# A decoder trunk's feed-forward: down as seven products, on PSUM chains of two banks a half

## The chip, the cores and the metric

One core of a Trainium2 chip runs the whole kernel in one launch. The metric is the device time of that launch in microseconds (us). PE is the matrix engine, DVE the vector engine, ACT the scalar engine, POOL the GpSimd engine, and SP the engine whose queue issues most loads. Each runs its own instructions in the order in which they were built.

## The reference

One step of a two-layer decoder: layer 0 mixes tokens by an mLSTM, layer 1 by latent attention, and each layer ends in a SwiGLU feed-forward with residual. There are 1024 prompt tokens and 8 sample tokens, which the kernel takes together (T = 1032). The change touches the feed-forward alone:

```python
D_MODEL = 1024
D_FF = 2816
def swiglu(x, w_gate_up, w_down):
    g, u = jnp.split(x @ w_gate_up, 2, axis=-1)
    return (jax.nn.silu(g) * u) @ w_down
...
hp = hp + swiglu(rmsnorm(hp, norm_ffn[layer]), ffn_w_gate_up[layer], ffn_w_down[layer])
hs = hs + swiglu(rmsnorm(hs, norm_ffn[layer]), ffn_w_gate_up[layer], ffn_w_down[layer])
```

All data are float32.

## The kernel before

**Precision.** Every float32 operand of a matmul is split into a high part (rounded by ACT) and a low part (the rest, subtracted by DVE or POOL): `split`. One product is then three matmuls, high by high, high by low, low by high: `mm3`. The letters h and l at the end of a tile's name are these parts.

**Gate and up.** The 2816 hidden rows are 22 blocks of 128. For one block `f`, the weights are two raw tiles of 128 by 1024 (gate `a11, a12` and up `a21, a22`, by even and odd rows of the model dimension). The tokens are cut into two halves `i` (512 and 520), each half into two quarters of 256 or 260. `forms` makes seven combinations of the normalised activations once a layer, `operands` makes seven of the weights for each block (sums on POOL: `L1000` to `L1009`), and `gate_up` multiplies them pair by pair: seven products take the place of eight (a fast matrix product of two by two blocks). Each product is 4 x 3 matmuls of 256 or 260 columns. Then the quarters are put together by additions on DVE, `silu` on ACT, and the product with up: tile `u`, which is split into `ah`, `al`.

**Down.** The hidden blocks are taken in pairs (`f0`, `f0 + 1`), since each pair's result is added to the residual `x_d` in memory by an accumulating DMA. `down` is a generator: one step is one chunk of 344 tokens of one output tile (`d` of 8), 2 blocks x 3 matmuls, then an eviction to `st` by ACT; after three chunks POOL issues the accumulating DMA. 24 steps are a pair. `gate_up` of the next blocks calls `next(down)` after each half product, which lays the down matmuls between the gate matmuls on PE.

**The edges.** In each layer blocks 0 and 1 run for half 0 ahead of the loop as plain products (`gate_up_half`, in `out_proj`) and for half 1 inside `ffn`. The last four blocks are not in the loop's down but in the products that follow: `to_mla` in layer 0, `finish` in layer 1, where the last gate block is also run one half after the other, so that half 0 can go on.

**What sets the order.** The program is recorded through pools of tiles with a fixed number of buffers (`bufs`), and instructions are placed on each engine's list by a scheduler at build time. At run time each engine follows its list and waits on semaphores. PSUM has eight banks under three names, `sc` (4), `mm` (2) and `ss` (2).

## Time and profile before

| | us |
|---|---|
| median of 3 runs (lowest, highest) | 2751.73 (2743.95, 2754.61) |
| the profiled execution | 2762.2 |
| its span | 2760.4 |
| PE busy | 2588.2 (94%) |
| DVE, ACT, POOL busy | 1495.5, 1178.5, 876.8 |

The first feed-forward runs from about 540 to 1250 us of the span, the second from about 2030 to the end. In the profile's rows, a group is a line of the code, an engine, an operation, `out<-in` tile names and the shape, then a count, the busy time and the mean ns of one, and behind the second bar the engine's idle time just before and what ended it. In a timeline row the first number is the start and the second the duration, both in us. Line numbers are those of the kernel before; the same helpers stand three lines lower in the changed one (`L131` is `L134` there, `L115` is `L118`).

### The profile page before, as it was taken

The page shows a single profiled execution, that of the slowest core. Times are in us where ns is not written, and L with a number is a line of the kernel's source. Part 1 is how long each engine was busy: PE and PEld are TensorE (multiplying, and loading weights), DVE is VectorE, ACT ScalarE, POOL GpSimd, SP SyncE. Part 2 cuts the span into 40 slices and gives each one's busy share as a digit, 9 for nine tenths or more (in the row PEclk, how much of TensorE's full clock was granted, in tenths as well). Part 3 has the DMA queues.
Part 4 walks back from the last instruction along what each step waited for, and adds up shares of the span by engine and source line. Part 5 has one row for each costly group of instructions (what it writes and reads, how often), then busy time and mean ns, then how long its engine had stood idle before and what let it go on. Part 6 is the DMA issues. An engine that isn't in the chain of part 4 may idle for free.

```text
span 2760.4 us, 52158 instructions
## 1 busy us (share of the span) xinstructions
PE 2588.2 (94%) x20719; PEld 2438.5 (88%) x20719; DVE 1495.5 (54%) x3217; ACT 1178.5 (43%) x2651; POOL 876.8 (32%) x846
## 2 busy tenths in 40 slices
PE   8999988989999999999988888798989999999998
PEld 8998977989999999999875667676888999999998
DVE  4345668863343443366557776677574444434445
ACT  4212334444444444443344455446344444444443
POOL 1001002233333333332334444442223333333343
PEclk9999989999999999999989999999999999999999
DMA  5133454526566556552666766654533666565653
GB/s 184 39 76 93 124 143 116 158 58 129 119 123 122 116 114 125 101 163 96 230 222 237 245 231 218 217 202 123 176 102 88 126 117 122 119 118 117 118 129 112
DMA packets 345210, 384.29 MB, mean 139 GB/s; under 512 B 24601, under 2 KB 296350, under 8 KB 336646
## 3 DMA queue, kind: packets, MB, share of 16 engines
q0 software_dynamic: 41088, 183.34, 27.7%
q1 hardware_dynamic: 279478, 181.26, 22.5%
q10 hardware_dynamic: 24400, 16.36, 2.4%
q8 instruction: 163, 2.67, 0.4%
q14 instruction: 81, 0.66, 0.1%
HBM read 255.17 MB, written 125.70 MB: 138 GB/s over the span
## 4 chain that ended last, share of the span: by engine, by line
PE 69%; DVE 13%; DMA 8%; ACT 4%; issue 4%; POOL 2%; another core or an unknown queue 0%; SPq 0%; ACTq 0%; POOLq 0%; DVEq 0%
PE sc L133 10%; PE sc L131 10%; PE sc L132 9%; PE mm L131 5%; PE mm L133 5%; PE mm L132 5%; PE ss L131 5%; PE ss L132 5%; PE ss L133 5%; DMA Gb<-G_d 2%; DVE tt L1700 2%; PE ss L1732 2%; PE ss L1707 2%; DVE wl L115 2%; PE mm L1603 1%
## 5 line engine op out<-in xcount | busy, mean ns | idle before, releaser
L131 PE MATMUL ss<-ah,dh 128*128 128x344 f32 x864 | 276.7, 320 | 6.0 <-ACT st L1075 5.6
L1075 ACT COPY st<-ss 128x344 f32<-128x344 f32 x432 | 190.2, 442 | 211.8 <-PE ss L133 182.5
L132 PE MATMUL ss<-al,dh 128*128 128x344 f32 x864 | 276.7, 320 | 1.9 <-POOL al L115 1.9
L133 PE MATMUL ss<-ah,dl 128*128 128x344 f32 x864 | 275.9, 319 | 0.0
L114 ACT ACTIVATE wh<-wr 128x512 fp32r<-128x512 f32 (+2 forms) x152 | 126.0, 830 | 229.0 <-PE mm L132 132.9
L1077 POOL DMA_DIRECT2D x_d<-st x144 | 125.4, 871 | 237.1 <-ACT st L1075 230.1
L131 PEld LDWEIGHTS ss<-ah,dh 128*128 128x128 f32 x864 | 162.5, 188 | 7.0 <-ACT st L1075 6.1
L115 POOL TENSOR_TENSOR al<-u,ah 128x512 fp32r<-128x512 f32 (+1 forms) x84 | 118.4, 1410 | 146.5 <-ACT ah L114 146.3
L132 PEld LDWEIGHTS ss<-al,dh 128*128 128x128 f32 x864 | 162.7, 188 | 2.4 <-POOL al L115 2.4
L115 DVE TENSOR_TENSOR wl<-S,wl 128x512 fp32r<-128x512 f32 x89 | 77.4, 870 | 158.0 <-ACT wl L114 130.3
L133 PEld LDWEIGHTS ss<-ah,dl 128*128 128x128 f32 x864 | 162.3, 188 | 0.0
L1700 DVE STREAM_TRANSPOSE tt<-nat 128x1024 f32<-128x1024 f32 x128 | 154.1, 1223 | 12.1 <-PE ss L1707 8.0
L1041 DVE TENSOR_TENSOR u<-u,sc 128x260 f32<-128x260 f32 (+1 forms) x168 | 70.7, 421 | 115.4 <-PE sc L133 114.1
L115 DVE TENSOR_TENSOR wh<-S,wh 128x512 fp32r<-128x512 f32 x91 | 68.2, 749 | 118.7 <-ACT wh L114 90.8
L115 DVE TENSOR_TENSOR wl<-wr,wh 128x1024 fp32r<-128x1024 f32 (+2 forms) x83 | 100.1, 1206 | 43.1 <-ACT wh L114 35.8
L1007 POOL TENSOR_TENSOR S<-S,wr 128x512 f32<-128x512 f32 x45 | 62.9, 1398 | 174.4 <-DVE wl L115 88.1
L1000 POOL TENSOR_TENSOR S<-wr 128x512 f32<-128x512 f32 x45 | 62.0, 1378 | 168.3 <-DMA wr<-in_ffn_w_gate_up_dram 157.7
L131 PE MATMUL mm<-zh,wh 128*128 128x344 f32 x320 | 105.3, 329 | 8.5 <-DVE ot L459 8.5
L1707 PE MATMUL ss<-tt,qbd 128*32 128x128 f32 x2560 | 95.4, 285 | 16.2 <-DVE tt L1700 10.9
L115 DVE TENSOR_TENSOR dl<-dr,dh 128x256 fp32r<-128x256 f32 x144 | 69.2, 481 | 71.4 <-ACT dh L114 71.4
L133 PE MATMUL mm<-zh,wl 128*128 128x344 f32 x320 | 104.5, 327 | 0.0
L132 PE MATMUL mm<-zl,wh 128*128 128x344 f32 x320 | 104.5, 327 | 0.0
(920 smaller groups left out, 9243.9 us busy)
## 6 DMA issues: line engine op xcount, KB each, us to landing
x_d<-st POOLq DMA_DIRECT2D x144, 516.0 KB
wr<-in_ffn_w_gate_up_dram SPq DMA_DIRECT2D x98, 512.0 KB
dr<-in_ffn_w_down_dram SPq DMA_DIRECT2D x144, 128.0 KB
wr<-in_mlstm_w_in_dram SPq DMA_DIRECT2D x24, 512.0 KB
wr<-in_mlstm_w_out_dram SPq DMA_DIRECT2D x16, 512.0 KB
wr<-in_mla_w_o_dram SPq DMA_DIRECT2D x15, 512.0 KB
q<-qn_d SPq DMA_DIRECT2D x28, 256.0 KB
x_d<-x SPq DMA_DIRECT2D x16, 260.0 KB
```

What stands on the lines that cost most here:

```text
L114: ins = nc.scalar.activation(hi, src, AF.Copy)
L115: self.low = e.tensor_tensor(lo, src, hi.bitcast(F32), op=ALU.subtract)
L131: mm(ps, wh, xh, start=start, stop=False, **kw)
L132: mm(ps, wh, xl, start=False, stop=False, **kw)
L133: self.last = mm(ps, wl, xh, start=False, stop=stop, **kw)
L1000: G(s, a21, a22, op=ALU.add)
L1007: G(s, s, a11, op=ALU.subtract)
L1041: V.tensor_tensor(u[:, 1], u[:, 1], ps, op=ALU.add)
L1075: nc.scalar.copy(st[:, cs], ps)
L1077: nc.gpsimd.dma_start(self.x_d[:, d], st, accum_op=ALU.add)
L1700: V.transpose(out=tt, in_=src.rearrange("p s (c i) -> p c s i", i=32))
L1707: nc.tensor.matmul(psS[32 * j:32 * j + 32, u * P:u * P + P], self.qbd[:, b, cb], tt[:, c, 4 * j:4 * j + 4].rearrange("p s k -> p (s k)"), ...
```

## The change

Down is now made by seven products too, for a pair of blocks and two output tiles (`dp` of 4) at a time. For this each pair's `u` (two blocks x two quarters of a half) is turned into seven sums, one tile each (`b0` to `b6` and the half's number), and the down weights into seven (`dA` to `dD`, two forms in each but `dD`). The scheme is the one of `PRODUCTS`, now used for gate and for down: two PSUM banks a half, products 0, 3, 2 and 5 in bank 0 and 4, 1 and 6 in bank 1. Inside a bank a product may add to what the one before left, and after it the bank is copied out as one of the four outputs. A down step is one product of one half, 3 matmuls of 256 or 260 columns; 14 steps are a group (`dp`), 56 a pair. A group ends in one accumulating DMA a half (2 x 512 or 2 x 520 columns). `SPREAD` says at which step of a pair each activation sum (`t1` to `t4`, in place in `u`) and each form of the next pair is made: entries 44 to 55 run in the last 12 steps of the pair before, and 56 to 60 in its own first five.

The loop's down now takes ten pairs a layer, and only the last two blocks are left to `to_mla` and `finish`. `gate_up` calls the down generator twice a half product. Weight forms of gate rotate through three buffers (`wh` twice, `w3`), not four; raw tiles have two (`wr`), not three; the two `wl` buffers now hold down's results of half 0.

```diff
-PRODUCTS = ((0, "a", 1), (1, "b", 1), (4, "a", 0), (2, "c", 1), (5, "b", 0), (3, "d", 1), (6, "c", 0))
-BANK = {"a": "sc", "b": "sc", "d": "sc", "c": "mm"}
+PRODUCTS = ((0, 0, 1), (4, 1, 1), (3, 0, 0), (1, 1, 1), (2, 0, 0), (5, 0, 0), (6, 1, 0))
+PARTS = {0: ("A", 0), 4: ("A", 1), 3: ("B", 0), 1: ("B", 1), 2: ("C", 0), 5: ("D", 0), 6: ("C", 1)}
+SPREAD = ((44, 0, 0), (45, 0, 1), (45, "t1", 0), (46, "t1", 1), (48, 4, 0), (49, 1, 0), (50, 1, 1), (51, 4, 1),
...
+          (56, 2, 1), (57, 5, 0), (58, 6, 0), (59, 5, 1), (60, 6, 1))
...
     def operands(self, wg, f):
...
         G(s, a21, a22, op=ALU.add)
         G(s3, a11, a21, op=ALU.subtract)
         yield put(a11)
+        yield put(a12)
+        s1 = put(s)
+        G(s, s, a11, op=ALU.subtract)
         yield put(s)
-        yield put(a12)
+        yield s1
+        G(s, a12, s, op=ALU.subtract)
         yield put(s3)
         yield put(a22)
-        G(s, s, a11, op=ALU.subtract)
         yield put(s)
-        G(s, s, a12, op=ALU.subtract)
-        yield put(s)
...
     def gate_up(self, wg, f, parts, down=iter(()), skip=0, steps=1):
...
                 for k in range(4):
                     self.mm3(ps, w[:, 0, k], w[:, 1, k], xh[:, k], xl[:, k], bool(first) and k == 0, k == 3, skip_group_check=True)
+                    if k % 2:
+                        if skip:
+                            skip -= 1
+                        else:
+                            for _ in range(steps):
+                                next(down, None)
...
+                    nc.scalar.copy(u[:, 0], ps)
+                elif s == 4:
+                    V.tensor_tensor(u[:, 0], u[:, 0], ps, op=ALU.add)
+                    nc.scalar.activation(u[:, 0], u[:, 0], AF.Silu)
+                elif s == 3:
+                    nc.scalar.copy(x, ps)
+                elif s == 2:
                     nc.scalar.copy(u[:, 1], ps)
+                    V.tensor_tensor(u[:, 1], u[:, 1], banks[i, 1], op=ALU.add)
+                elif s == 5:
+                    V.tensor_tensor(u[:, 0], u[:, 0], ps, op=ALU.mult)
+                elif s == 6:
+                    V.tensor_tensor(x, x, ps, op=ALU.add)
+                    nc.scalar.activation(x, x, AF.Silu)
+                    V.tensor_tensor(u[:, 1], u[:, 1], x, op=ALU.mult)
...
+    def spread(self, f0, n, i):
+        V, G = self.nc.vector, self.nc.gpsimd
+        a = self.u[f0, i]
+        b = self.u.get((f0 + 1, i))
+        if n == "t1":
+            G.tensor_tensor(a[:, 0], a[:, 1], a[:, 0], op=ALU.subtract)
+        elif n == "t2":
+            V.tensor_tensor(a[:, 0], b[:, 1], a[:, 0], op=ALU.subtract)
+        elif n == "t3":
+            G.tensor_tensor(a[:, 1], b[:, 1], a[:, 1], op=ALU.subtract)
+        elif n == "t4":
+            G.tensor_tensor(b[:, 0], b[:, 0], a[:, 0], op=ALU.subtract)
+        else:
+            x = a[:, n // 2] if n < 4 and n != 3 else a[:, 0] if n == 3 else b[:, n // 6]
+            w = self.t(self.fp, [P, 2, PW[i]], f"b{n}{i}", F32R)
+            self.split(w[:, 0], w[:, 1], x, lo_eng=V if n in (3, 5) else G)
+            self.B[n, i] = w
...
+    def down_raw(self, wd, f0, dp):
...
+        raw = self.t(self.fp, [P, 2, 2 * P], "dr")
+        nc.sync.dma_start(raw, self.wsrc(wd, f0 * P, 2, dp * 2 * P, 2 * P))
...
+        S = self.t(self.fp, [P, 4, P], "dS")
+        G(S[:, 1], a21, a22, op=ALU.add)
+        G(S[:, 0], S[:, 1], a11, op=ALU.subtract)
+        G(S[:, 2], a11, a21, op=ALU.subtract)
+        G(S[:, 3], a12, S[:, 0], op=ALU.subtract)
...
+    def down(self, wd):
...
+            for e in range(14):
+                s, k, first = PRODUCTS[e // 2]
+                i = e % 2
+                ps = banks[i][k]
+                w, j = PARTS[s]
+                w, b = W[w][:, :, j], self.B[s, i]
+                self.mm3(ps, w[:, 0], w[:, 1], b[:, 0], b[:, 1], bool(first), True, skip_group_check=True)
...
+                elif s == 6:
+                    V.tensor_tensor(c[:, 0, 1], c[:, 0, 1], ps, op=ALU.add)
+                    nc.gpsimd.dma_start(self.x_d[:, 2 * dp:2 * dp + 2, 512 * i:512 * i + 2 * PW[i]], st[i], accum_op=ALU.add)
+                if more and e == 0:
+                    src = self.down_raw(wd, *todo[n + 1])
+                if more and e in (6, 9, 12, 13):
+                    x = {6: "A", 9: "B", 12: "D", 13: "C"}[e]
+                    W[x] = self.down_put(src, x)
+                for f, z in ((f0, dp * 14 + e + 56), (f0 + 2, dp * 14 + e)):
+                    if 0 < f < NF - 2:
+                        for when, x, part in SPREAD:
+                            if when == z:
+                                self.spread(f, x, part)
                 yield
```

How this stands on the engines is shown at three places. A row is line, operation, `out<-in` with buffer numbers, and shape.

The first place is POOL in the middle of a layer, in gate block 7 and the start of block 8. Before: `S` are gate's weight sums, `al` the low half of a `u`, `x_d<-st` the accumulating DMAs.

```order
L115 TENSOR_TENSOR al21087_7336<-u1094_7361,ah21086_7335 128x512
L115 TENSOR_TENSOR al21087_7336<-u1097_7377,ah21086_7335 128x520
L1077 DMA x_d10_91<-st1135_7674 128x1032
L1009 TENSOR_TENSOR S1141_7689<-S1141_7689,wr21139_7685 128x512
L1077 DMA x_d10_91<-st1157_7768 128x1032
L1000 TENSOR_TENSOR S1196_8071<-wr21195_8069 128x512
L1001 TENSOR_TENSOR S1197_8072<-wr1194_8067,wr21195_8069 128x512
L1077 DMA x_d10_91<-st1166_7843 128x1032
L1007 TENSOR_TENSOR S1196_8071<-S1196_8071,wr1194_8067 128x512
```

Now, from the second activation sum of half 1 on (`L1073` and `L1075` are t3 and t4, `dS` the sums of down's weights, `b21` the second form of half 1, `S1171` the sums of block 8):

```order
L1073 TENSOR_TENSOR u011095_7647<-u111139_8047,u011095_7647 128x260
L1141 DMA x_d10_91<-wl908_6158 128x2x512
L1141 DMA x_d10_91<-st1153_8214 128x2x520
L1075 TENSOR_TENSOR u111139_8047<-u111139_8047,u011095_7647 128x260
L1090 TENSOR_TENSOR dS1188_8458<-dr1187_8456 128x128
L1092 TENSOR_TENSOR dS1188_8458<-dr1187_8456 128x128
L1091 TENSOR_TENSOR dS1188_8458<-dS1188_8458,dr1187_8456 128x128
L118 TENSOR_TENSOR b211189_8463<-u011095_7647,b211189_8463 128x260
L1093 TENSOR_TENSOR dS1188_8458<-dr1187_8456,dS1188_8458 128x128
L118 TENSOR_TENSOR b601195_8496<-u101129_8011,b601195_8496 128x256
L118 TENSOR_TENSOR b611198_8525<-u111139_8047,b611198_8525 128x260
L1012 TENSOR_TENSOR S1171_8392<-S1171_8392,wr1169_8388 128x512
```

`L1012` (sum - a11, before `L1007`) stood one DMA behind the block's first sums; now a DMA pair, a t4, four `dS` and three `b` stand directly ahead of it.

The second place is PE in block 8, where that difference is used (`wh1227` before, `w31200` now; `f3` is the activation form it meets). Before, in the sixth product:

```order
L133 MATMUL sc1207_8127<-c5h830_5583,wl1224_8248 128x260
L131 MATMUL ss1226_8283<-ah21086_7335,dh1220_8235 128x344
L132 MATMUL ss1226_8283<-al21087_7336,dh1220_8235 128x344
L133 MATMUL ss1226_8283<-ah21086_7335,dl1221_8236 128x344
L131 MATMUL ss1226_8283<-ah31137_7683,dh1220_8235 128x344
L132 MATMUL ss1226_8283<-al31138_7684,dh1220_8235 128x344
L133 MATMUL ss1226_8283<-ah31137_7683,dl1221_8236 128x344
L131 MATMUL sc1228_8296<-f3h783_5207,wh1227_8293 128x256
```

Now, in the third product:

```order
L136 MATMUL sc1197_8514<-c4h828_5574,wh1193_8482 128x260
L134 MATMUL mm1185_8450<-b311178_8433,dB1166_8350 128x260
L135 MATMUL mm1185_8450<-b311178_8433,dB1166_8350 128x260
L136 MATMUL mm1185_8450<-b311178_8433,dB1166_8350 128x260
L134 MATMUL sc1174_8399<-f3h783_5207,w31200_8544 128x256
```

A down step is three matmuls of 260 columns in place of six of 344, and the product of the difference has moved from sixth to third.

The third place is SP at the end of layer 1, where `finish` loads the residual (`f6h`, `f7h` are its row tiles 6 and 7) and the last down weights (`wr`). Before:

```order
L1807 DMA wr4654_30194<-in_ffn_w_down_dram 128x4x128
L1815 DMA gB4666_30245<-in_norm_final_dram 128x1024
L1802 DMA f7h4647_30178<-x_d10_91 128x384
L1813 DMA f7h4647_30178<-x_d10_91 128x384
L1807 DMA wr4656_30200<-in_ffn_w_down_dram 128x4x128
L1807 DMA wr4658_30206<-in_ffn_w_down_dram 128x4x128
```

Now:

```order
L1903 DMA wr4566_32606<-in_ffn_w_down_dram 128x2x128
L1903 DMA wr4568_32612<-in_ffn_w_down_dram 128x2x128
L1898 DMA f6h4558_32589<-x_d10_91 128x384
L1903 DMA wr4570_32618<-in_ffn_w_down_dram 128x2x128
L1898 DMA f7h4559_32590<-x_d10_91 128x384
L1903 DMA wr4572_32624<-in_ffn_w_down_dram 128x2x128
```

Four of the eight weight loads now stand behind the load of `f6h`, which waits for the last pair's accumulating DMA.

More of the change, by code (lines that the diff above doesn't have):

```diff
@@ L1027, in gate_up @@
                 pw = PW[i]
-                if first:
-                    banks[i, bank] = self.mmt(BANK[bank])[:, :pw]
+                if (i, bank) not in banks:
+                    banks[i, bank] = self.mmt("sc")[:, :pw]
                 ps = banks[i, bank]
@@ L1047, in gate_up @@
-                if s == 6:
-                    V.tensor_tensor(g[:, 1], u[:, 1], ps, op=ALU.subtract)
-                    nc.scalar.activation(g[:, 1], g[:, 1], AF.Silu)
-                    V.tensor_tensor(u[:, 1], u[:, 1], g[:, 1], op=ALU.mult)
-                    o = lambda x: x[:, 512 * i:512 * i + 2 * pw].rearrange("p (c t) -> p c t", c=2)
-                    self.split(o(ah), o(al), u, lo_eng=nc.gpsimd)
-                if skip:
-                    skip -= 1
-                else:
-                    for _ in range(steps):
-                        next(down, None)
@@ L1138, in to_mla @@
         tl.release()
+        self.lt.release()
         self.gu.release()
```

152 lines of the change are left out of this document (90 added, 62 removed).

## The prediction

> **What bounds the kernel now.** First the page's busy line and then the windows of the two feed-forward stages (columns: stretch, PE, weight loads, DVE, ACT, POOL, granted clock, DMA share, GB/s).
>
> ```profile
> PE 2588.2 (94%) x20719; PEld 2438.5 (88%) x20719; DVE 1495.5 (54%) x3217; ACT 1178.5 (43%) x2651; POOL 876.8 (32%) x846
> ...
> 900.00:1000.00 100.00, 100.00 (x770) 100.00 (x769) 42.02 (x86) 45.55 (x101) 36.01 (x32) 1.00 0.58 114
> ...
> 1200.00:1230.00 30.00, 29.90 (x190) 29.62 (x189) 20.62 (x39) 18.69 (x38) 13.08 (x14) 1.00 0.70 227
> ...
> 2200.00:2300.00 100.00, 100.00 (x771) 100.00 (x770) 40.66 (x81) 43.10 (x96) 36.16 (x32) 1.00 0.58 114
> ```
>
> In the steady stretch of either layer PE never rests, at full clock, and the other engines have half their time free. So time there is matmul issue time, and only fewer or shorter matmuls can lower it, as long as the others keep up. What one matmul costs is read from the starts in the timeline of PE, since its records overlap: the rows below open, in turn, 12 matmuls of 256 columns, 6 of 344, 12 of 260, and the next 344.
>
> ```profile
> 801.61 0.28 PE L131 MATMUL sc<-f3h,wh 128*128 128x256 f32 x1
> ...
> 803.03 0.32 PE L131 MATMUL ss<-ah,dh 128*128 128x344 f32 x1
> ...
> 803.98 0.28 PE L131 MATMUL sc<-c3h,wh 128*128 128x260 f32 x1
> ...
> 805.42 0.32 PE L131 MATMUL ss<-ah,dh 128*128 128x344 f32 x1
> ```
>
> (803.03-801.61)/12 = 0.118 us, (803.98-803.03)/6 = 0.158, (805.42-803.98)/12 = 0.120.
>
> **The gain in PE.** Down takes blocks in pairs. Before, a pair is 8 output tiles x 3 chunks x 2 blocks x 3 = 144 matmuls of 344 columns: 22.8 us. Now it is 4 x 7 products x 2 halves x 3 = 168 of 256 or 260: 20.0 us. That is 2.8 us a pair; of 20 pairs (10 a layer, where before 9 ran in the loop and one more in the tail), 55 us. The trace's spacing grows with the columns, and the sum goes by that. [...]
>
> **Small terms.** Waits of PE in the stretches 585:1260 and 2080:2760 (us, times, longest):
>
> ```profile
> PE ss L131 <- ACT st L1075: 3.0, 1, 3.0
> PE sc L131 <- ACT u L1039: 3.4, 3, 1.5
> PE ss L131 <- ACT st L1075: 2.7, 1, 2.7
> ```
>
> The two `st` waits are the first down pair at double rate, with two `st` buffers behind an accumulating DMA (below, 7.42 us). Now a buffer comes back after two groups of 14 steps, some 20 us: +5.7. At the start of each layer and in the layer 1 block done half by half, bank 0 is copied by ACT and written by the very next product: 6 such turns of about 0.9 (the longest of those waits is 1.5 and the mean 1.1), and the single-half blocks need the second POOL difference at their third product, not their sixth, from two raw buffers, not three: -5 together, where nothing excludes -12 or 0.
>
> The tail of layer 0 halves its PE work (two blocks left, not four), 0.94 us a chunk. Its other work does not shrink:
>
> ```profile
> 1212.23 0.58 ACT L117 ACTIVATE f2h<-x,g 128x344 fp32r<-128x344 f32 x1 [0.92 <-DVE x L1127]
> 1212.72 0.48 ACT L1133 ACTIVATE sq<-x 128x344 f32<-128x344 f32 x1
> ...
> 1212.85 0.58 DVE L118 SCALAR_TENSOR_TENSOR f2l<-x,g,f2h 128x344 fp32r<-128x344 f32 x1 [0.65 <-ACT f2h L117]
> 1213.59 0.51 DVE L1127 TENSOR_TENSOR x<-x,sc 128x344 f32<-128x344 f32 x1 [0.16 <-PE sc L133]
> ```
>
> A chunk takes ACT 1.06 and DVE 1.09, plus a weight split per tile: about 1.2 us against 0.94, so 24 chunks give back 6.2. In layer 1 the last pair's accumulating DMA now lands after the last gate block, and SP holds the fifth weight load behind the load of row tile 6, which waits for it:
>
> ```profile
> 622.99 7.42 DMA x_d<-st
> ...
> 2696.88 4.43 DMA wr<-in_ffn_w_down_dram
> ```
>
> Two steps and evictions 2 us, 7.4, 4.4, a split 1, and the next two weights 4: the first third of the final products ends near 19 us, where its 8 x 6 matmuls of 384 columns (0.175, from the spacings) need 8.4. With DVE's share of the other thirds, -12.
>
> Without any new wait in the loop: 55 + 5.7 - 5 - 6.2 - 12 = 37.5, some 37 us faster.
>
> **What the loop now asks of the others.** Per instruction, steady stretch, then nearest rows from the whole run:
>
> ```profile
> L1075 ACT COPY st<-ss 128x344 f32<-128x344 f32 x203 | 89.6, 442 | 97.9 <-PE ss L133 87.3 <-issue 5.4 <-DMA x_d<-st 3.8
> L1077 POOL DMA_DIRECT2D x_d<-st x68 | 59.2, 871 | 109.3 <-ACT st L1075 107.1 <-PE sc L133 2.2
> L115 DVE TENSOR_TENSOR wl<-S,wl 128x512 fp32r<-128x512 f32 x36 | 31.7, 881 | 67.6 <-ACT wl L114 40.5 <-PE ss L133 27.2
> L114 ACT ACTIVATE dh<-dr 128x256 fp32r<-128x256 f32 x66 | 27.4, 415 | 32.1 <-PE ss L132 30.7
> L115 POOL TENSOR_TENSOR al<-u,ah 128x512 fp32r<-128x512 f32 x18 | 26.1, 1448 | 36.4 <-ACT ah L114 36.4
> L1009 POOL TENSOR_TENSOR S<-S,wr 128x512 f32<-128x512 f32 x18 | 23.2, 1290 | 59.9 <-DVE wh L115 36.7 <-DVE wl L115 20.9 <-PE sc L133 2.3
> L114 ACT ACTIVATE wl<-S 128x512 fp32r<-128x512 f32 x36 | 22.7, 630 | 22.1 <-PE sc L133 19.0 <-PE mm L133 3.1
> L1041 DVE TENSOR_TENSOR u<-u,sc 128x256 f32<-128x256 f32 x36 | 15.1, 419 | 17.6 <-PE sc L133 17.6
> ...
> L1039 ACT COPY u<-sc 128x256 f32<-128x256 f32 x40 | 14.3, 357 | 5.1 <-PE sc L133 4.0 <-POOL al L115 1.1
> ...
> L631 POOL TENSOR_TENSOR qw<-q,wb 128x256 f32<-128x256 f32 x14 | 10.6, 762 | 132.5 <-PE sc L641 93.0 <-DMA wb<-wi_d 26.7 <-DMA Gb<-G_d 12.7
> ...
> L283 POOL MEMSET ones<- 128x128 f32 x1 | 0.2, 222 | 0.0
> ```
>
> A pair was 336 x 0.119 + 22.8 = 62.8 us and is to be 60. POOL had 36% of it, 22.6 us. It gains 6 activation sums and 10 low halves of 256 (0.76 each), 16 weight sums of 128 columns, and loses 4 `al` of 1.45. For 128 columns the trace has no such row: between the memset's 0.22 and 0.76 I take 0.48, on the line through 256 and 512 columns (0.76, 1.29). 22.6 + 12.2 + 7.7 - 5.8 = 37 us, 61%. ACT goes from 28 to about 39 (32 evictions of 0.36 for 24 of 0.44, 14 high halves of 0.415 for 4 of 0.63, more weight halves, 8 more gate evictions), DVE from 26 to about 40 (24 adds of 0.42 in down, 20 in gate). None is the bound by its mean; POOL's work comes in a lump.
>
> **The lump.** The seven forms of a pair's activations are made while the pair before ends and the next even gate block starts. That block's third product multiplies (sum - a11), whose second POOL subtraction, L1012, stands on POOL behind the lump (in the order quoted ahead). Count from the last down step before it. PE has 36 gate and 18 down matmuls until the third product: 54 x 0.119 = 6.4 us. POOL's path: DVE's add after that step 0.42 with 0.25 of hand-over, the DMA's issue 0.87, one activation sum 0.76, three weight sums 1.44, a low half 0.76, a fourth weight sum 0.48 with two more low halves 1.52, L1012 1.29, ACT's high half 0.63, DVE's low half 0.88: 8.4 us to the high half and 9.3 to the low, which is needed two matmuls later. That is 2.0 us of wait for the high half and then 0.6 for the low, 2.6. One thing more is late: DVE reaches that add behind `u` multiplied by its silu, and ACT's silu stands behind three high halves that wait for POOL's own sums (0.76 each plus hand-overs). I walk that to about 1 us. So 3.5 us.
>
> Below: weight sums as short as the memset (0.22) save 1.0 of the four, and the hand-overs and the last delay may vanish: 1.0. Above: DVE runs slow beside POOL:
>
> ```profile
> 801.58 0.69 DVE L115 TENSOR_TENSOR wl<-S,wl 128x512 fp32r<-128x512 f32 x1 [3.97 <-ACT wl L114]
> ...
> 810.37 1.62 POOL L115 TENSOR_TENSOR al<-u,ah 128x512 fp32r<-128x512 f32 x1
> ...
> 811.10 1.45 DVE L115 TENSOR_TENSOR wl<-S,wl 128x512 fp32r<-128x512 f32 x1 [0.30 <-ACT wl L114]
> ```
>
> 0.69 became 1.45, and POOL's 1.45 became 1.62. With three or four such meetings on the path, 5.5. I take 3.5, since it is built from rows of the same operations, most of them averages that hold some contention. [...]
>
> There are 8 even blocks a layer with this order (6 to 20), 16 in all: 56 us. In block 4 the subtraction stands before most of the lump; 1.7 in each layer: 3.4. Sum: 37 gained, 59 lost, 22 slower. The profiled execution lasted 2762.2 us (span 2760.4), 10.5 above the median of 2751.73; 2762.2 + 22 = 2784, and on the scale of the runs 2774.
>
> **The rivals.** *The lump is absorbed* (POOL's sums are short, waits under 1 us): 2752 - 37 + 0 to 16 = 2715 to 2731, faster. For it speaks POOL's mean of 61%; against it the count above, where only the unmeasured 128-column sums can give much. It decides below a mean wait of 1.4 us. *Break-even*: the wait is the bare 2.0 to 2.6 minus shorter weight sums, about 2.1: 34 lost, 2755, the same. *The banks turn too slowly*: in a down half, product 2 is copied out of bank 0 by ACT and product 5 writes it two steps later, 1.8 us; 12 such turns a pair with gate's, over 200 in all. At 0.3 us each that is 65 us instead of the lump: 2780; beside it, 2835. For it: ACT at 65% in order; against: a copy takes 0.36, and the steps' other turns have 4 us. It cancels the gain from 0.18 us a turn on. That the change does not do what it says has no chance, since the order shows 168 short matmuls a pair.
>
> **Chances.** Forecast 0.46, absorbed 0.26, break-even 0.17, banks 0.11. Half a per cent, about what these runs can tell from no change (their spread is 0.4%), is 14 us: faster 0.26, same 0.17, slower 0.57. The range 2718 to 2818 reaches down to the absorbed case and up to waits of 5.5 with some bank turns. The forecast alone: 2752 to 2806.
>
> **What would show it.** Right: PE idle, some 3 to 4 us, once per pair at the third product of even blocks, released by ACT or DVE on the weights of that product, with POOL full just before; starts still 0.118 apart elsewhere; the tail of layer 0 with DVE and ACT as releasers. Wrong: PE at 100% over a whole pair (absorbed), or many short waits for `wl`, `st` or `u` copies spread over the pair (banks). If PE idles at POOL's weight sums `dS` or at raw loads instead, the place is wrong though the sign may hold.

## The result, and the profile after

The changed kernel takes 2919.28 us (median of 4 runs, 2909.79 to 2930.27) beside 2752.78 for the kernel before (4 runs): a ratio of 1.0613, 95% interval 1.0569 to 1.0657. The forecast was 2774, with 2818 as the upper end: the sign was right, the size far off. The busy line of the page after, and two windows of its feed-forward loops:

```profile
PE 2605.7 (89%) x21199; PEld 2438.1 (84%) x21199; DVE 1891.6 (65%) x3825; ACT 1357.2 (47%) x3403; POOL 1246.2 (43%) x1422
```

```profile
660.60:1207.00 546.40, 503.46 (x4034) 497.42 (x4033) 357.45 (x638) 282.90 (x766) 318.06 (x381) 0.95 0.55 109
...
2230.00:2780.00 550.00, 503.87 (x4022) 496.85 (x4022) 364.55 (x635) 282.12 (x763) 314.09 (x378) 0.95 0.55 109
```

PE now rests 43 to 46 us in each loop, and the granted clock over the loop is 0.95. Before, the two numbers were 0 and 1.00. In layer 0 odd blocks take 30.0 us, as forecast for a loop without waits; even blocks from 6 on take 38.4 to 40.7. These waits of PE stand in blocks 4 to 19 of layer 0:

```profile
PE sc L134 <- ACT wh L117: 19.5, 5, 6.6
PE mm L135 <- DVE b L118: 16.3, 6, 5.1
PE sc L134 <- ACT w L117: 6.4, 2, 5.2
```

The first and third are the third product, as forecast. The second was not forecast: a low half of `b` on DVE, which the down step just ahead of the third product waits for. One stall of the first kind, in PE's timeline:

```profile
730.75 0.28 PE L136 MATMUL mm<-b,dB 128*128 128x260 f32 x1
736.22 0.58 PE L134 MATMUL sc<-f3h,wh 128*128 128x256 f32 x1 [5.18 <-ACT wh L117]
...
737.32 0.41 PE L134 MATMUL sc<-f3h,wh 128*128 128x256 f32 x1
...
740.96 0.42 PE L136 MATMUL sc<-c3h,wh 128*128 128x260 f32 x1
...
741.52 0.28 PE L136 MATMUL sc<-c3h,wh 128*128 128x260 f32 x1
741.63 0.28 PE L134 MATMUL mm<-b,dC 128*128 128x256 f32 x1
```

After the wait of 5.18 us the starts are (740.96 - 737.32)/17 = 0.214 us apart, and 0.118 again only from 741.5 on. Windows around it show why (the column before the DMA share is the granted clock):

```profile
731.00:736.20 5.20, 0.03 (x1) 0.00 (x0) 3.33 (x5) 1.66 (x5) 4.50 (x7) 0.84 0.88 150
736.20:739.60 3.40, 3.38 (x14) 3.16 (x15) 2.61 (x3) 1.44 (x4) 1.29 (x1) 0.50 0.06 14
739.60:743.00 3.40, 3.40 (x24) 3.40 (x23) 0.84 (x2) 1.26 (x4) 0.00 (x0) 0.74 0.49 147
743.00:750.00 7.00, 7.00 (x61) 7.00 (x61) 3.41 (x9) 4.04 (x11) 2.60 (x4) 1.00 0.28 48
```

The clock falls to 0.5 while PE stands still and stays there behind it: 0.50 x 3.4 + 0.26 x 3.4 = 2.6 us of PE time lost behind this wait. Wait and low clock together, 7.8 us, are what this block, of 38.6 us, has over 30, but for 0.3 at `b` and some smaller gaps. Over both loops 16.6 us of the clock's loss fell into PE's waits themselves, where it costs nothing (clock rows at 0.5 while PE is idle, summed from the trace). POOL in the same place, with the accumulating DMAs, t4, the sums `dS` and L1012:

```profile
728.15 1.20 POOL L1141 DMA_DIRECT2D x_d<-st  x1 [0.20 <-issue]
728.92 1.21 POOL L1075 TENSOR_TENSOR u<-u,u 128x260 f32<-128x260 f32 x1
...
732.51 1.77 POOL L118 TENSOR_TENSOR b<-u,b 128x256 fp32r<-128x256 f32 x2
733.89 1.61 POOL L1012 TENSOR_TENSOR S<-S,wr 128x512 f32<-128x512 f32 x1
```

And a stall of the second kind, on DVE, POOL and ACT:

```profile
934.61 6.82 DVE L118 TENSOR_TENSOR b<-u,b 128x260 fp32r<-128x260 f32 x1
941.34 0.41 DVE L1131 TENSOR_TENSOR wl<-wl,ss 128x256 f32<-128x256 f32 x1
...
934.27 1.20 POOL L1141 DMA_DIRECT2D x_d<-st  x1 [0.21 <-issue]
...
939.80 1.33 POOL L1012 TENSOR_TENSOR S<-S,wr 128x512 f32<-128x512 f32 x1
...
941.51 0.38 ACT L1047 COPY u<-sc 128x260 f32<-128x260 f32 x1 [4.80 <-DVE b L118]
```

A subtraction of 260 columns, 0.42 us elsewhere, lasts 6.82: it begins during POOL's DMA issue and ends 0.3 us after POOL's last instruction of the run, at 941.13. DVE's adds and ACT's copies queue behind it.

By stretches the 155.6 us between the two spans (2916.0 and 2760.4) are: to the start of block 4, +4.4; blocks 4 to 19 of layer 0, +44.7; from there to block 4 of layer 1, +29.5; blocks 4 to 19 of layer 1, +50.3; the rest, +26.7. (The medians are 166.5 us apart, since the profiled execution of the kernel before lay 9.4 us above its median.)

### The profile page after: what moved, and what is told of

It reads as the page before. It is cut to its first block, busy times and chain, and to the rows that moved or that the text cites. A ratio compares the mean times of both kernels' runs of the same rounds, so it can differ in the third digit from the quotient of the medians.

```text
span 2916.0 us, 55167 instructions
## 1 busy us (share of the span) xinstructions
PE 2605.7 (89%) x21199; PEld 2438.1 (84%) x21199; DVE 1891.6 (65%) x3825; ACT 1357.2 (47%) x3403; POOL 1246.2 (43%) x1422
## 4 chain that ended last, share of the span: by engine, by line
PE 53%; DVE 16%; DMA 10%; POOL 8%; issue 7%; ACT 5%; SPq 0%; another core or an unknown queue 0%; ACTq 0%; POOLq 0%; DVEq 0%
PE sc L134 9%; PE sc L136 9%; PE sc L135 9%; PE mm L134 4%; PE mm L136 4%; PE mm L135 4%; DMA wr<-in_ffn_w_gate_up_dram 3%; POOL b L118 2%; DVE tt L1796 2%; PE ss L1828 2%; DMA Gb<-G_d 2%; PE ss L134 1%; PE ss L135 1%; PE ss L136 1%; DVE b L118 1%
## 5 line engine op out<-in xcount | busy, mean ns | idle before, releaser
L117 ACT ACTIVATE wh<-wr 128x512 fp32r<-128x512 f32 (+3 forms) x176 | 139.0, 790 | 225.9 <-PE mm L135 129.4
L1141 POOL DMA_DIRECT2D x_d<-wl x80 | 96.1, 1202 | 324.0 <-DVE wl L1140 285.4
L118 POOL TENSOR_TENSOR b<-u,b 128x256 fp32r<-128x256 f32 (+1 forms) x200 | 176.5, 918 | 28.8 <-ACT b L117 28.8
L117 ACT ACTIVATE b<-u 128x256 fp32r<-128x256 f32 (+1 forms) x280 | 110.0, 413 | 119.2 <-POOL u L1073 40.1
L118 DVE TENSOR_TENSOR b<-u,b 128x256 fp32r<-128x256 f32 (+1 forms) x80 | 115.2, 1454 | 22.7 <-ACT b L117 22.7
L1007 POOL TENSOR_TENSOR S<-wr 128x512 f32<-128x512 f32 x45 | 63.7, 1415 | 128.1 <-DMA wr<-in_ffn_w_gate_up_dram 113.1
L118 DVE TENSOR_TENSOR wh<-wr,wh 128x512 fp32r<-128x512 f32 x91 | 90.5, 996 | 29.4 <-ACT wh L117 28.8
L118 DVE TENSOR_TENSOR dB<-dS,dB 128x256 fp32r<-128x256 f32 x80 | 58.8, 735 | 68.0 <-ACT dB L117 68.0
L1012 POOL TENSOR_TENSOR S<-S,wr 128x512 f32<-128x512 f32 x45 | 63.8, 1417 | 86.8 <-DVE wh L118 66.0
L1803 PEld LDWEIGHTS ss<-tt,qbd 128*32 128x32 f32 x2560 | 72.2, 112 | 32.6 <-DVE tt L1796 18.9
L117 ACT ACTIVATE wh<-S 128x512 fp32r<-128x512 f32 x121 | 76.2, 630 | 43.0 <-PE sc L136 24.4
L130 POOL TENSOR_TENSOR wl<-spl,wh 128x512 fp32r<-128x512 f32 x43 | 54.8, 1285 | 76.7 <-ACT spl L129 72.1
```

The costliest lines, as they stand in the source:

```text
L117: ins = nc.scalar.activation(hi, src, AF.Copy)
L118: self.low = e.tensor_tensor(lo, src, hi.bitcast(F32), op=ALU.subtract)
L130: nc.gpsimd.tensor_tensor(lo, x, hi.bitcast(F32), op=ALU.subtract)
L1007: G(s, a21, a22, op=ALU.add)
L1012: G(s, s, a11, op=ALU.subtract)
L1141: nc.gpsimd.dma_start(self.x_d[:, 2 * dp:2 * dp + 2, 512 * i:512 * i + 2 * PW[i]], st[i], accum_op=ALU.add)
```

## The experiments

The theory: POOL's backlog in even blocks and the low clock after each stall. Rivals: DVE standing still beside POOL; the banks; the tails. All ratios are to the kernel before.

**Gate's order alone in the old kernel** (its chain, evictions and product order; down, four weight buffers and three raw ones as before).

```diff
-PRODUCTS = ((0, "a", 1), (1, "b", 1), (4, "a", 0), (2, "c", 1), (5, "b", 0), (3, "d", 1), (6, "c", 0))
+PRODUCTS = ((0, 0, 1), (4, 1, 1), (3, 0, 0), (1, 1, 1), (2, 0, 0), (5, 0, 0), (6, 1, 0))
...
```

> The kernel before with gate alone changed: its seven products as a chain in two banks a half with the evictions of the changed kernel, the difference as third product; down as before in chunks of 344, four weight buffers, three raw ones. Theory: gate's new order and evictions cost nothing by themselves, since POOL has no lump here: PE without waits in blocks 4 to 19, 2745 to 2760. Rival (PSUM banks turn too slowly: product 5 writes bank 0 one half product after 2 is copied): 80 such turns of 0.3 us or more, 2775 or more.

2737.83 us, ratio 0.9958 (0.9937 to 0.9979). Blocks 4 to 19 last 501.7 us without a wait, as before, and block 4 begins at 642.7 instead of 656.2 (two other runs with the old order, shown further down, begin it at 647.6 and 650.9, so a part of that is variation between executions). So half of the change is harmless, even good by some 12 us, and the rival of slow banks is out for gate. This is the only version here that beats both kernels; the loss comes with down and with the fewer buffers that go with it.

**A later third product.**

```diff
+GATE = tuple(PRODUCTS[i] for i in (0, 1, 3, 2, 4, 5, 6))
...
-        for (s, bank, first), w in zip(PRODUCTS, self.operands(wg, f)):
+        for (s, bank, first), w in zip(GATE, self.operands(wg, f)):
```

> Gate takes the product of the plain weight sum third and that of (sum - a11) fourth; what stands on POOL and the down steps are as in the changed kernel, so that L1012 has 36 matmuls (4.3 us) more time. Theory (POOL's lump delays L1012, and each stall of about 5 us is followed by a clock of one half that costs 3.4 us more): in the 5 of 8 even blocks a layer whose stall stands at the third product 5.2 to 6.6 us become 1 or 2, and their clock loss goes; the other three (5.15 us at the low half of `b`, DVE) lose only the 1.2 us at the third product. About 40 us a layer, 2830 to 2850. Rival (the activation forms are what is late, and the third product only the first to show it): the same stall comes a few matmuls later at `b`, 2900 to 2925.

2913.62, ratio 1.0593 (1.0566 to 1.0621): next to nothing. The waits of PE from 690 to 1160 us:

```profile
PE sc L135 <- DVE u L1051: 25.3, 12, 5.6
PE mm L135 <- ACT wl L1137: 10.8, 6, 2.1
PE mm L136 <- DVE b L119: 6.9, 6, 5.1
```

The weights are no longer waited for, but the add of `u` that frees gate's bank 1 now stands late in DVE's queue. To take L1012 off the path was not enough.

**Matmuls to hold the clock.** 42 matmuls that nobody reads, ahead of the stall in the even blocks 6 to 20; first into gate's bank 1, then into unused columns of bank 0.

```diff
...
+                    if s == 4 and i and k == 3 and f % 2 == 0 and 4 < f < NF - 1:
+                        for q in range(42):
+                            nc.tensor.matmul(full[0, 0][:, 264:512], w[:, 0, 0], self.F[0][4][0][:, 0, :248], start=False, ...)
```

> 42 matmuls of 256 columns that compute nothing that is read (5.0 us) are laid ahead of the stall in each of the even blocks 6 to 20, into a PSUM bank that is free there. Theory (the stall of 5.2 us is a wait for POOL and DVE, and the granted clock falls because PE stands still): the stall is filled, the clock stays at 1.0 through blocks 4 to 19, the waits for POOL stay where they were in time, and each even block loses 3.4 us: 16 x 3.4 = 55 us, 2865. Rival (the clock falls for another reason, the heavier mix of work on the other engines, say): the clock falls all the same, and the time is 2915 to 2930.

> The 42 matmuls that compute nothing read (248 columns, 4.9 us, ahead of the stall in the even blocks 6 to 20) now write the unused columns of a bank that nobody has yet to read, so they wait for nothing; in the earlier form they waited for the add of `u` on DVE and so came after the stall. Theory (the granted clock falls because PE stands still for 5 us): the stall is filled, the clock stays 1.0 in blocks 4 to 19, each even block is 35 to 36.5 us instead of 38.4 to 40.7: 16 x 3.4 = 55 us, 2865. Rival (the clock falls for another reason): even blocks as before or longer, 2915 to 2935.

The first took 2977.6, ratio 1.0794 (1.0716 to 1.0872): its matmuls themselves waited 6.25 us for DVE's add of `u` on that bank, and so came behind the stall. The second took 2909.3, ratio 1.0558 (1.0504 to 1.0611), not the 2865 expected. The loop of layer 0:

```profile
657.40:1201.30 543.90, 528.75 (x4328) 522.64 (x4327) 360.17 (x637) 282.19 (x766) 317.29 (x381) 0.98 0.55 110
```

The clock did hold: summed over its rows, the loss in blocks 4 to 19 falls from 28.4 and 29.0 us in the two layers to 8.5 and 11.4. That part of the theory stands. The time followed by 10 us only, and the two loops together by 7.6. Of the clock's loss 16.6 us had fallen into the waits, where it costs nothing; and the stall's end moved, since DVE's subtraction now stood long in most blocks (6.89 us in block 6): filled and idle time together grew from 89 to some 100 us. Those two give back about 28 of the 37. So the run shows that PE's standing still brings the low clock about, but not that the time follows when the clock is held.

**Activation sums and their low halves on DVE.**

```diff
-        V, G = self.nc.vector, self.nc.gpsimd
+        V = G = self.nc.vector
```

> All activation sums and all low halves of `b` on DVE; POOL keeps the weight sums and the DMAs. Theory (POOL's lump): t4 and three low halves, some 3.6 us, no longer stand ahead of L1012, the stall falls from 5.2 us to 1 or 2, and the low clock after it goes: 16 x (3.5 + 3.4) = 110 us, about 2810. Rival (DVE, busy 65% and slow beside POOL, becomes the late one): it gains some 7 to 10 us of work a pair, `b` and the adds come later, the stall moves to `b` or to `st` and stays 4 to 6 us: 2900 to 2960.

2817.81, ratio 1.0248 (1.0218 to 1.0278), 101 us less, as the theory said. Even blocks from 6 on take 32 to 35 us and wait here:

```profile
PE sc L136 <- DVE wh L118: 11.9, 5, 2.5
PE sc L136 <- DVE w L118: 4.5, 2, 2.5
```

**The sums `dS` on DVE as well.**

```diff
     def down_raw(self, wd, f0, dp):
-        G = nc.gpsimd.tensor_tensor
+        G = nc.vector.tensor_tensor
```

> As the run with the activation sums and low halves on DVE, and the sums of down's weights (dS) on DVE too; POOL keeps gate's weight sums and the DMAs. Theory (a DVE subtraction of two SBUF tiles cannot go on while POOL works through a burst without a gap; and DVE is in order): the 2 us in which `b` stood still beside POOL's four dS go, but DVE gains 4 x 0.28 of its own; the low half of the third product's weights, which stands behind them, comes some 0.5 us sooner, so 2.5 us of wait become 2.0: 2790 to 2815. Rival (POOL's backlog alone is the cause): there is no lump left on POOL, no wait in even blocks, 2745 to 2765.

2801.55, ratio 1.0159 (1.0112 to 1.0206). The waits of 2.5 become 1.2, and no low clock is left in layer 0's loop; its blocks 4 to 19 take 503.1 us, a tie with the 501.7 before. What remains is DVE's order.

**With all of that on DVE and another order of the products, in gate and down, and in gate alone.**

```diff
-PRODUCTS = ((0, 0, 1), (4, 1, 1), (3, 0, 0), (1, 1, 1), (2, 0, 0), (5, 0, 0), (6, 1, 0))
+PRODUCTS = ((0, 0, 1), (4, 1, 1), (1, 1, 1), (3, 0, 0), (2, 0, 0), (5, 0, 0), (6, 1, 0))
...
```

> The same, and the product of the plain weight sum third, that of the difference fourth, in gate and in down (one swap in the list of products). Theory (what is left in the even blocks is DVE's order, 2 to 2.5 us late at the third product): 4.3 us more time for those weights covers it, no stall of over 1 us in blocks 4 to 19, full clock there; against the run with the activation sums on DVE 52 us of idle time and 24 us of low clock in blocks 4 to 19 go: 2745 to 2770. Rival (PSUM bank 1 is now turned two steps after product 4, and the add that frees it stands in DVE's queue): waits for `u` or `st` adds of 1 to 3 us a pair, 2775 to 2830.

> All activation sums, their low halves and the dS on DVE, and the product of the plain weight sum third in gate alone; down keeps the order of the changed kernel, so that its banks are turned as there. Theory (the 1.2 us left in each even block at the third product are DVE's order in front of that product's low half): they are covered by 4.3 us more time, 16 x 1.2 = 19 us, 2780 to 2785. Rival (gate's bank 1 waits for the add of `u`, as in the earlier run with this order): 0.5 to 3 us in each even block, 2795 to 2830.

The second run swaps by `GATE`, as above. Both rivals came, the first beyond its range: 2898.25 (ratio 1.0527, 1.0477 to 1.0576) and 2809.71 (1.0195, 1.0152 to 1.0238). The loop of layer 0 takes 545.8 us in the first, as much as in the changed kernel, by a bank turn of two steps:

```profile
PE ss L134 <- DVE wl L1132: 47.8, 31, 3.0
```

That is the rival "banks turn too slowly" of the forecast, at 1.5 us a turn; it is real once an add in DVE's queue frees a bank, but it is not what the changed kernel suffers from.

**The sums `dS` alone on DVE** (the edit of `down_raw` above), POOL's order otherwise unchanged.

> The changed kernel with nothing but the four weight sums dS of down moved from POOL to DVE; POOL's order is otherwise the same, its DMA issues, t4 and three low halves still ahead of L1012. Theory (POOL's backlog at the even blocks sets the stall): its four sums took 2.2 to 2.9 us there, L1012 comes that much sooner, the stall of 5.2 to 6.3 us becomes 3 us or a little more, and the low clock after it one or two of the pieces of 1.7 us less: 16 x (2.5 + 1.2) = 60 us, about 2860. Rival (the lock of DVE's subtraction sets the stall and lasts as long as POOL has work without a gap, DMA issue and t4 included): the sums on DVE stand behind it too, the stall stays over 4.5 us, 2890 to 2925.

2924.6, ratio 1.0616 (1.0593 to 1.064): the rival. L1012 ends 1.9 us sooner in its block, yet PE waits 3.5 us at `b` and 1.1 to 1.4 at the third product, and the even blocks 6 to 18 of layer 0 still take 38.3 to 39.2 us. Block 6 on DVE:

```profile
729.25 5.20 DVE L118 TENSOR_TENSOR b<-u,b 128x260 fp32r<-128x260 f32 x1
734.36 0.28 DVE L1090 TENSOR_TENSOR dS<-dr 128x128 f32<-128x128 f32 x1
```

DVE stands until POOL's run is over, and the four sums and the third product's low half come behind.

**The low halves of `b` all on POOL.**

```diff
-            self.split(w[:, 0], w[:, 1], x, lo_eng=V if n in (3, 5) else G)
+            self.split(w[:, 0], w[:, 1], x, lo_eng=G)
```

> The changed kernel with all low halves of `b` on POOL, those of forms 3 and 5 too, so that no DVE subtraction of `b` stands beside POOL's backlog, which grows by two low halves ahead of L1012. Theory A (the backlog sets the stall, and DVE's 2 to 6.8 us long subtraction only decides who is named): L1012 comes 1.7 us later, 16 x 1.7 = 27 us, 2935 to 2950. Theory B (DVE standing still in that subtraction, with the adds and ACT's copies queued behind it, sets the stall): the stall falls by 1 to 3 us, 2860 to 2900.

2938.59, ratio 1.0679 (1.064 to 1.0718), as theory A said. Nothing of `b` stands still on DVE, and the backlog alone gives 6.4 us:

```profile
PE sc L134 <- ACT wh L117: 25.6, 4, 6.4
PE sc L134 <- ACT w L117: 12.8, 2, 6.4
```

So there are two routes of nearly one length: through L1012 at the backlog's end, and through DVE, which the backlog holds until that end. To shorten one does not help.

**Without the accumulating DMAs.**

```diff
-                    nc.gpsimd.dma_start(self.x_d[:, 2 * dp:2 * dp + 2, 512 * i:512 * i + 2 * PW[i]], st[i], accum_op=ALU.add)
```

> The changed kernel without down's accumulating DMAs, so that the residual lacks ten pairs of blocks in each layer. Theory (POOL's backlog at the even blocks sets the stall, and two issues of 1.2 us are part of it): L1012 comes 2.4 us sooner, the stall of 5.2 us becomes 2.8, with less low clock after it, and the tail's first loads need not wait: 16 x (2.4 + 1.0) + 10 = 65 us, about 2855. Rival (the issues are not on the path, since POOL would wait for `u` and its sums in that time): 2900 to 2915. If the long subtractions on DVE are caused by the issue (each began during one), they are short here, under 1.5 us.

2792.94, ratio 1.0145 (1.0115 to 1.0176), 126 us less, twice what was expected. Blocks 4 to 19 of layer 0 take 499.8 us; the third product's wait is gone and one of 2.0 us is left:

```profile
PE mm L134 <- ACT st L1129: 13.9, 7, 2.1
```

The longest DVE subtraction between 700 and 900 us is 1.81 us. But the scheduler, with no issue to place, also put L1012 ahead of the four `dS`. How much of the 126 us belongs to the issues and how much to that order is not separated.

**A POOL burst by itself**, in the kernel before, in three forms. The third:

```diff
+BURST = {7: 8, 9: 16, 11: 24, 13: 32}
...
         G(s3, a11, a21, op=ALU.subtract)
+        if f in BURST and f > 3:
+            scr = [self.t(self.gu, [P, P], f"scr{q}") for q in range(2)]
+            for q in range(BURST[f]):
+                G(scr[q % 2], s3[:, q % 4], a11[:, q % 4], op=ALU.subtract)
```

> The kernel before, with sums on POOL that nobody reads (128 columns of SBUF, back to back) after the third product of four odd gate blocks in each layer: 4 in block 7, 8 in 9, 16 in 11, 32 in 13, alone some 0.55 us each, 2.2, 4.4, 8.9 and 17.8 us. Theory (a DVE subtraction of two SBUF tiles waits until POOL's burst ends): a DVE low half begun in the burst lasts up to 2, 4, 9 and 18 us, DVE's adds from PSUM keep their 0.42, and PE idles in blocks 11 and 13 for what goes beyond its slack (5 us or more in 13), 15 to 30 us longer in all. Rival (DVE and POOL share the bandwidth): no DVE low half over 1.5 us, POOL's sums at up to 1.1 us, PE without waits, the time of the kernel before.

> The kernel before, with extra POOL sums that nobody reads (128 columns, of a weight sum and a raw weight, back to back behind L1001 and L1002) in four odd gate blocks of each layer: 8 in block 7, 16 in block 9, and the same behind one more DMA issue in blocks 11 and 13. Theory 1 (a DVE subtraction of two SBUF tiles stands until POOL has a gap): DVE subtractions of 3 to 6 us in blocks 9 and 13, 2 to 3 us in 7 and 11, each ending with the burst. Theory 2 (it needs a DMA issue at its start): such ones in blocks 11 and 13 alone. Theory 3 (the two only share the bandwidth): none above 1.5 us in any of the four.

> As the second burst, but the extra sums write two tiles in turn, so that none waits for the one before and POOL's records overlap as in the backlog of the changed kernel: 8 in block 7, 16 in 9, 24 in 11, 32 in 13. Theory 1 (a DVE subtraction of two SBUF tiles gets through only in a gap between POOL's instructions; the second burst had gaps of 0.08 us after each sum): subtractions of 3 us and more that end with the burst, in 9, 11 and 13. Theory 2 (they share the bandwidth, and something else holds DVE in the changed kernel): none above 1.5 us.

The first burst was placed ahead of the loop as one piece and says little of what was asked: DVE's subtractions beside it rose from about 1.23 to 1.43 us (time 2787.23, one run). In the second (2751.95, one run), with 0.08 us between the sums, none stood: theory 3. The third (2768.8, one run) has the case. DVE and POOL in block 13:

```profile
930.70 0.42 DVE L1050 TENSOR_TENSOR u<-u,sc 128x256 f32<-128x256 f32 x1
931.15 7.15 DVE L1051 TENSOR_TENSOR u<-u,gt 128x256 f32<-128x256 f32 x1
...
929.65 0.87 POOL L1082 DMA_DIRECT2D x_d<-st  x1
930.25 6.51 POOL L1006 TENSOR_TENSOR scr<-S,wr 128x128 f32<-128x128 f32 x15
936.52 1.49 POOL L1012 TENSOR_TENSOR S<-S,wr 128x512 f32<-128x512 f32 x1
```

A product of two SBUF tiles, 0.52 us in the second burst, lasts 7.15 us, until 0.3 us behind the end of POOL's last sum, and 7.14 in layer 1. The add from PSUM just before it keeps its 0.42. Subtractions that met the same burst ahead of the DMA issue got through in 0.7 to 1.0 us, though POOL had no gap there either. What differs is how POOL's records lie: ahead of the issue each overlaps the next by 0.04 us, behind it by 0.3. From 640 to 1240 us every stretch of POOL with overlaps of 0.2 us or more begins right behind a DMA issue: 22 in the changed kernel, 10 in the kernel before, 14 here. The subtraction dA of block 6 in the changed kernel had no issue near, but it stood in such a stretch, which began with the issue at 728.15 and ended at 735.50:

```profile
733.28 2.52 DVE L118 TENSOR_TENSOR dA<-dr,dA 128x256 fp32r<-128x256 f32 x1 [1.47 <-ACT dA L117]
```

The run without the accumulating DMAs has no such stretch, and from 640 to 1240 us no DVE subtraction of two SBUF tiles lasts over 1.81 us in it, though POOL works there for 8 us without a gap. That speaks for the issue as what starts the long wait. It is not isolated: that run also moved L1012, and in two other runs some such stretches begin behind short sums or copies.

**Gaps in the backlog.** A copy of one column behind each of POOL's steps:

```diff
...
+    def gap(self, x):
+        self.nc.gpsimd.tensor_copy(self.tiny, x[:, 0:1])
```

> The changed kernel with one more POOL copy of a single column behind each of its activation sums, low halves and dS, each of which waits for the end of what it copies: small gaps in the backlog, some 0.1 us more work each. Theory 1 (DVE needs a gap on POOL): the subtraction of b in the even blocks falls from 2 to 6.8 us to under 2.5, the stall from 5.2 to 6.3 us to 3 or 4, about 2870. Theory 2 (gaps do not matter): the stall as before or 0.5 us longer, 2919 to 2940.

2960.15, ratio 1.0772 (1.0743 to 1.0801). It made no gaps: the scheduler moved copies, POOL's records still overlap, the subtraction of `b` lasts 5.03 us, and the backlog only grew. Inconclusive on gaps.

**The tail of layer 0**, its down weights as two tiles ahead of the residual's loads.

```diff
+        G4 = [self.load_w(self.wsrc(wd, fs[0] * P, len(fs), d * P, 4 * P), len(fs), 4 * P) for d in (0, 4)]
         for d in range(KT):
-            w = self.load_w(self.wsrc(wd, fs[0] * P, len(fs), d * P, P), len(fs), P)
+            w = tuple(x[:, :, d % 4 * P:d % 4 * P + P] for x in G4[d // 4])
```

> The kernel with everything on DVE and gate's swap, and in layer 0 the last down weights are loaded and split as two tiles of 512 columns ahead of the residual's loads, not as eight of 128 between its loads and stores. Theory (the tail of layer 0 gave nothing back because PE waits for weights that stand in SP's queue behind the residual, and the clock falls for it: 11 us of idle time and 8 us of low clock): 10 to 15 us below the run without it. Rival (DVE's 1.25 us a chunk and the residual's own transfers set the tail): 0 to 4 us below.

> Everything on DVE, the order of products as in the changed kernel, and the last down weights of layer 0 as two tiles ahead of the residual's loads. From the run without the two tiles (2801.6) and the 13.7 us that this stretch lost in the trace with them: 2788. If the two tiles only shift the wait to the residual's transfers: 2797 to 2803.

2802.45 (1.0188, 1.0163 to 1.0214) beside 2809.71, and 2790.69 (1.0122, 1.0092 to 1.0152) beside 2801.55, for the two kernels above with everything on DVE (gate's swap, and the first order). By the times alone the two tiles could be nothing, since the intervals overlap. In the traces the stretch from block 20 to block 4 of layer 1 loses 13.7 and 14.0 us. PE's waits in the tail without and with the two tiles:

```profile
PE sc L137 <- DVE wl L119: 9.2, 4, 4.0
PE sc L135 <- ACT wh L118: 3.5, 2, 1.8
```

```profile
PE sc L135 <- DVE x L1225: 4.8, 4, 2.7
PE mm L135 <- DVE x L1225: 1.1, 1, 1.1
```

So the late weights cost the tail these 14 us (the edit moves their loads ahead and makes two of eight; which of the two did it is not told apart). DVE's residual adds are what is left.

## Why the prediction was wrong in size

**The gain in PE** was right: 30.0 us a block, 60.0 a pair where no wait stands, starts 0.118 apart.

**The lump** was the right place, and in 7 of the 16 even blocks from 6 on the right releaser; in the other nine the long wait stands one down step ahead, at the low half of `b`, with 1.2 us more at the third product. It was undersized: 3.5 us forecast, 4.9 to 6.6 measured with both waits counted, 5.9 in the mean, and in nine blocks over the 5.5 of its upper bound. The step that failed is the way to the first of POOL's steps. In block 6 the last down step ended at 723.86 and its add on DVE at 727.63, 3.8 us later, where I had 0.42, 0.25 and the "about 1 us", 1.67 together. (The 0.25 of hand-over was an estimate that no row shows: in the kernel before, DVE's add of `u` starts at 803.23, 0.04 behind the end of PE's record.) Over the 16 blocks it is 2.2 to 5.0 us, 3.9 in the mean, and the issue starts another 0.5 behind the add.

```profile
723.57 0.29 PE L136 MATMUL ss<-b,dC 128*128 128x260 f32 x1
...
727.22 0.41 DVE L1140 TENSOR_TENSOR st<-st,ss 128x260 f32<-128x260 f32 x1
...
735.53 0.63 ACT L117 ACTIVATE wh<-S 128x512 fp32r<-128x512 f32 x1 [1.98 <-POOL S L1012]
```

The steps behind it were priced well: from the start of that issue (728.15) to the end of L1012 (735.50) it is 7.35 us, over the 16 blocks 6.9 to 7.6, and my terms from the issue to L1012 add up to 7.12. POOL's groups of that loop look dearer:

```profile
L1141 POOL DMA_DIRECT2D x_d<-st x32 | 43.5, 1360 | 1.3 <-ACT b L117 0.6 <-issue 0.6
L118 POOL TENSOR_TENSOR b<-u,b 128x260 fp32r<-128x260 f32 x39 | 35.6, 920 | 0.0
L1090 POOL TENSOR_TENSOR dS<-dr 128x128 f32<-128x128 f32 x32 | 25.7, 803 | 7.3 <-DMA dr<-in_ffn_w_down_dram 4.3 <-DVE w L118 1.2 <-DVE wl L1131 1.0
```

An issue lasts 1.36 us in the mean, a low half 0.92 and a `dS` 0.80, for my 0.87, 0.76 and 0.48. But these records overlap, and what a step adds is the distance of the starts: in block 6 0.77 us from the issue to t4 and 0.69 for each low half.

The add is late because POOL is late before the lump that I counted. In 14 of the 16 blocks it ends 11.1 to 11.2 us after the start of L1007, gate's first weight sum for the block. Behind that one stand L1008, four low halves, t3 and t4 of half 0; ACT's high halves wait for these sums, DVE's low halves for ACT, and the add comes behind them on DVE. In ten of the blocks L1007 itself had waited 0.6 to 1.9 us for the raw weights, of which the changed kernel holds two tiles, not three:

```profile
716.43 1.40 POOL L1007 TENSOR_TENSOR S<-wr 128x512 f32<-128x512 f32 x1 [0.67 <-DMA wr<-in_ffn_w_gate_up_dram]
```

This chain is read from the rows; no run moved L1007 or gave the third raw tile back.

**DVE beside POOL** I counted as three or four instructions of twice their length, 5.5 us at the worst. The rows show one instruction of 6.82, with everything behind it on DVE and then on ACT. The rows of the kernel before that I went by gave 1.45 for 0.69, and its longest DVE instruction from 640 to 1240 us is 1.84: none of them stands as the one of 6.82 does here and the one of 7.15 in the burst, until a run of several POOL instructions is over. The traces bear out the direction: the upper end of 5.5 lies nearer than 3.5 to the 5.9 measured in the mean.

**The clock** has no term in the forecast, and that is the largest miss. From the two traces' spans and mean clocks, 2916.0 x (1 - 0.946) - 2760.4 x (1 - 0.973) = 83 us more went to it, 57 of them in blocks 4 to 19, where the kernel before lost none. Of the 83, 25 fell into waits of PE (11.6 us before, 36.5 after):

```profile
core 0: 2916.0 us, clock 0.946
```

```profile
core 0: 2760.4 us, clock 0.973
```

A wait of 3.5 us was priced at 3.5, though the kernel before, in its stretch with waits at the start of layer 0, already showed the price:

```profile
540.00:580.00 40.00, 33.57 (x251) 32.86 (x250) 28.96 (x40) 17.22 (x27) 11.36 (x7) 0.87 0.19 55
```

The runs show the same: the clock is at 0.50 behind the stall of 5.18 us, and waits of 1.9 to 2.5 us lowered it too, behind 6 of 8 in the run with the activation sums alone on DVE; nothing was lost in layer 0's loop with waits of 1.2 us, in the run with everything on DVE. A low clock behind the waits should have been a rival.

**The small terms.** The tail of layer 0 was to give back 22.8 - 6.2 us and gave none: it waits for weights as shown, and its clock falls too. I had priced ACT's and DVE's work per chunk but not where SP's loads stand. The chain of waits after shows one of them:

```profile
1281.08 7.37 DMA wr<-in_ffn_w_down_dram
...
1293.99 3.80 DMA x<-x_d
```

The 1.7 us for block 4 had no working; the block took 31.0 and 31.4 us, 1.0 and 1.4 over 30. The stretch at the end of layer 1, with the two last blocks, was to cost 20 + 3.5 - 22.8 + 12 = 13 us and cost 26.7; the one from block 20 to block 4 of layer 1 cost 29.5. No experiment took the end of layer 1 apart.

**The sum**: 22 us forecast; 42 more for the stalls (89 us idle in blocks 4 to 19 and 12 in the two blocks 20, for 59); 83 - 25 = 58 for the clock behind waits, the tails' included; which leaves 34 of the 156 for the tails' own waits, the starts, and a smaller gain. Over the whole traces PE's idle time grew by 138 us (172 to 310) and the clock's loss beside it by 58, and what is left, the time in which matmuls go on, fell by 41, not 55. A part of that is waits that do not show: a matmul's record lasts 0.28 us and the starts are 0.118 apart, so a wait below some 0.16 us leaves no idle time.

Of the rivals "absorbed" and "break-even" fell; "banks" fell for this kernel and came true in the reordered one. Two of their times do not follow from their own terms: break-even is 2749 to 2752, not 2755, and banks beside the lump 2839, not 2835.

## What to carry to other kernels

The longer waits of PE cost more than themselves here: read the granted clock behind a wait. One of 5.2 us took 2.6 us more by the clock's rows, so my estimate for another of that length is about 8; but the run that held the clock saved only 10 us, so this is an account, not a saving on offer. A burst on one engine must be timed from where it begins on that engine's own list, with all that stands ahead of it, and by the starts of its rows, since their durations overlap (in block 6 an issue of 1.20 us, and t4 0.77 behind its start). Count with it every DVE instruction on two SBUF tiles that falls into it: two here ended only 0.3 us behind the burst, after 6.82 and 7.15 us, and what queued behind the first waited too (ACT's copy 4.80). Where two routes of the same length hold a stall, taking one away shows nothing: move work off the engine that both share, as the runs with the sums on DVE did.

## What the hardware showed unexpectedly

A DVE instruction on two SBUF tiles stood for 4.7 to 7.2 us beside a run of POOL instructions behind a DMA issue (0.42 to 0.52 without it), while instructions with a PSUM operand kept their 0.42. The granted clock stood at 0.50 for 3.4 us at a time (1.7 us lost each time), one to three times for a stall (twice behind the one of 5.18 us, from 734.5 to 741.4), and holding PE busy with matmuls that compute nothing kept the clock but saved only 10 us.
